# One block of scores moved one period ahead in a stick-breaking attention

## The chip, the cores and the metric

The kernel runs on one NeuronCore of a Trainium2 chip. The metric is the device time of one launch in microseconds (us). It is compared as a median of runs, and one further run was taken with the hardware profiler.

## The reference, cut to what matters

The kernel computes one layer of a decoder trunk on 1024 tokens of width 1024, all in 32-bit floats. It has a mixing sub-layer (stick-breaking attention beside a state-space mixer), a cross-attention and a feed-forward. The change is in the attention, which has 16 heads of width 64:

```python
for blk in range(seq // SB_BLOCK):               # 8 blocks of 128 rows
    t0 = blk * SB_BLOCK; t1 = t0 + SB_BLOCK
    z = einsum('bhtd,bhsd->bhts', qf[:, :, t0:t1], kf[:, :, :t1])
    causal = arange(t1)[None, :] < (t0 + arange(SB_BLOCK))[:, None]
    log_1mb = where(causal, log_sigmoid(-z), 0.0)
    tail = cumsum(log_1mb, axis=3, reverse=True)
    w = where(causal, exp(z + tail), 0.0)
    outs.append(einsum('bhts,bhsd->bhtd', w, vf[:, :, :t1]))
```

A block of 128 rows looks only at the keys up to its own end, so block 1 has 128 columns of scores, block 4 has 512, block 5 has 640 and block 8 has 1024.

## The kernel before, in words

Each head is worked off in two halves of four row blocks. A **short** half holds blocks 1 to 4 (128 to 512 columns), a **long** half holds blocks 5 to 8 (640 to 1024 columns). The 32 halves are numbered m = 0 to 31; even m is the short half of head m/2, odd m the long half of the same head.

For one row block, `scores` issues the score products on TensorE (L872, L873, in pieces of at most 512 columns into the three PSUM buffers `sc`), a sigmoid on ScalarE for each piece (L874, into the tile `n`), and one scan on VectorE over all the columns (L875). The `n` tiles of long halves come from a pool with four buffers, so a new block of a long half can be written only when the same block of the previous long half has been read for the last time.

For one half, `values` goes over key blocks i (four in a short half, eight in a long one). `tr(i)` transposes `n` on TensorE (L889, two PSUM buffers `tr`), ScalarE makes the high part `wth` (L892) and VectorE the low part `wtl` (L893). Three steps later `av(i)` multiplies both with the value differences (L901 with `wth`, L902 with `wtl`). So each L902 waits for a VectorE instruction.

A **period** m issues three things through `interleave`, which gives every item a place between 0 and 1 and sorts by it: the values of half m (over the whole period), the scores of half m+1 (over 0 to 0.7), and a quarter of the next two heads' q and k projections (`dense`, L104 to L106, spread over the whole period). In an even period the short values therefore stand beside the four long scans, and in an odd period the long values beside the four short ones.

This is the order in which the program is written. A scheduler places the instructions in each engine's queue by what it expects to be ready, and each queue then runs strictly in order. For two successive heads, first one with an even number and then one with an odd number, VectorE's queue holds the following. S5 to S8 are the long scans, s1 to s4 the short scans of the next head, w0 to w7 the `wtl` of the long values, v0 to v3 those of the short values after them, and gt and wlo the evacuation and the low weights of the projections:

```text
even head: w0 w1 w2 w3 gt S5 w4 w5 S6 S7 w6 w7 S8 s1 v0 s2 v1 wlo gt s3 v2 v3 s4
odd head:  w0 w1 w2 w3 gt S5 w4 w5 S6 S7 w6 w7 S8 s1 v0 v1 wlo gt s2 s3 v2 v3 s4
```

(In both rows S5 to S8 belong to the head after the one whose w's are listed.) ScalarE's sigmoids and TensorE's products stand in the order that this asks for. On GpSimd stand the value differences (`va`, L852, and their high and low parts, L94 and L101) and half of the high weights `whi`.

Of the kernel before, what the change touches and what calls it, by code (L numbers as in the profile page):

```python
# [34 lines left out]
def hybrid_block(ctx, tc, a, out, dbg=None):  # L35
# [13 lines left out]
    def mk(pl, shape, dt, tag, bufs=None):  # L49
        uid[0] += 1  # L50
        kw = {} if bufs is None else {"bufs": bufs}
        return pl.tile(shape, dt, tag=tag, name=f"{tag}_{uid[0]}", **kw)
# [202 lines left out]
    with ExitStack() as pa:  # L255
# [494 lines left out]
        with ExitStack() as p2:  # L750
# [85 lines left out]
            def gate_proj(gi):  # L836
                def ev(ps, half):
                    gt = mk(t2, [P, HALF], F32, "gt")
                    A.activation(gt, ps, AF.Sigmoid)
                    nc.sync.dma_start(g_d[gi * P:(gi + 1) * P, half * HALF:(half + 1) * HALF], gt)  # L840
                return dense(C_GA + gi * P, ev)
# [3 lines left out]
            def differences(h):  # L845

                j = h % 2
                if j == 0:
                    va, vb = [mk(vp, [P, NCH, P], F32, n, bufs=1) for n in ("va", "vb")]
                    for t, r in ((va, 0), (vb, 1)):  # L850
                        nc.sync.dma_start(t, v_d[r:S + r, h * HD:(h + 2) * HD].rearrange("(c p) d -> p c d", p=P))
                    G.tensor_tensor(va, va, vb, ALU.subtract)  # L852
                    dvs[0] = va
                dv = dvs[0][:, :, j * HD:(j + 1) * HD]
                vt = mk(vp, [P, NCH, P], F32R, "v")
                hi_sb(vt[:, :, 0:HD], dv, "p")
                lo_of(vt[:, :, HD:P], dv, vt[:, :, 0:HD], G)
                heads[h]["v"] = vt

            def scores(h, half, tb, ns_):  # L860
                def run():
                    hd = heads[h]
                    if half == 0 and tb == 0:
                        differences(h)
                    b = half * 4 + tb
                    L = (b + 1) * P
                    nt = mk(bp, [P, (half + 1) * HALF], F32, f"n{half}")
                    ns_.append(nt)
                    for s0 in range(0, L, HALF):
                        s1 = min(L, s0 + HALF)  # L870
                        ps = mk(psc, [P, HALF], F32, "sc")[:, :s1 - s0]
                        T.matmul(ps, hd["qs"][:, b * P:(b + 1) * P], hd["kh"][:, s0:s1], start=True, stop=False)  # L872
                        marks.append(T.matmul(ps, hd["qs"][:, b * P:(b + 1) * P], hd["kl"][:, s0:s1], start=False, stop=True))  # L873
                        sig.append(A.activation(nt[:, s0:s1], ps, AF.Sigmoid, scale=-(HD ** -0.5)))  # L874
                    V.tensor_tensor_scan(nt[:, 0:L][:, ::-1], nt[:, 0:L][:, ::-1], mask[:, S - L:][:, ::-1], 1.0, ALU.mult, ALU.max)  # L875
                return run
# [3 lines left out]
            def values(h, half, ns_):  # L880

                st = {}
                ni = 4 * (half + 1)

                def tr(i):
                    t0 = max(0, i - 4 * half)
                    pt = mk(pst, [P, HALF], F32, "tr")
                    for tb in range(t0, 4):
                        T.transpose(pt[:, tb * P:(tb + 1) * P], ns_[tb][:, i * P:(i + 1) * P], ident)  # L889
                    wh = mk(wt, [P, HALF], F32R, "wth")  # L890
                    wl = mk(wt, [P, HALF], F32R, "wtl")
                    A.activation(wh[:, t0 * P:], pt[:, t0 * P:], AF.Identity, bias=mone)  # L892
                    V.scalar_tensor_tensor(wl[:, t0 * P:], pt[:, t0 * P:], -1.0, wh[:, t0 * P:].bitcast(F32), ALU.add, ALU.subtract)  # L893
                    st[i] = (wh, wl, t0 * P)

                def av(i):
                    if i == 0:
                        st["po"] = mk(psv, [P, HALF], F32, "av")
                    po, vt = st["po"], heads[h]["v"]
                    wh, wl, off = st[i]  # L900
                    T.matmul(po[:, off:], vt[:, i, :], wh[:, off:], start=i == 0, stop=False)  # L901
                    marks.append(T.matmul(po[:, off:], vt[:, i, :], wl[:, off:], start=False, stop=i == ni - 1))  # L902
                    if i == ni - 1:
                        o = mk(t2, [P, HALF], F32, "oT")
                        A.activation(o, po, AF.Copy)
                        for j in range(2):
                            nc.sync.dma_start(o_d[j][h * HD:(h + 1) * HD, half * HALF:(half + 1) * HALF], o[j * HD:(j + 1) * HD])

                def step(i):
                    def run():  # L910
                        if i < ni:
                            tr(i)
                        if i >= LAG:
                            av(i - LAG)
                    return run

                return [step(i) for i in range(ni + LAG)]

            def interleave(*lists):
                items = []  # L920
                for n, (l, a0, a1) in enumerate(lists):
                    for i, f in enumerate(l):
                        items.append((a0 + (a1 - a0) * (i + 0.5) / len(l), n, f))
                for _, _, f in sorted(items, key=lambda t: t[:2]):
                    f()

            def qk_quanta(hp):

                if hp >= NH // 2:
                    return [[]] * 4  # L930
                q, k = qk_proj(hp)
                n = KT // FQ + 1
                return [q[:n], q[n:] + k[:1], k[1:n], k[n:]]
# [4 lines left out]
            NM = 2 * NH  # L938
            ns_ = {m: [] for m in range(NM)}
            nxt = qk_quanta(1)  # L940
            interleave(([scores(0, 0, tb, ns_[0]) for tb in range(4)], 0, 0.7), (nxt[0], 0, 1))
            late = [f for gi in range(16 - LATE_GATES, 16) for f in gate_proj(gi)]
            for m in range(NM):
                h, half = m // 2, m % 2
                hp, r = m // 4, m % 4
                s1 = [scores((m + 1) // 2, (m + 1) % 2, tb, ns_[m + 1]) for tb in range(4)] if m + 1 < NM else []
                if r == 3:
                    nxt = qk_quanta(hp + 2)
                dn = nxt[(r + 1) % 4]
                if m >= NM - 5:  # L950
                    n = -(-len(late) // (NM - m))
                    dn, late = late[:n], late[n:]
                interleave((values(h, half, ns_[m]), 0, 1), (s1, 0, 0.7), (dn, 0, 1))
            sig_last = sig[-1:]


# [946 lines left out]
```

## Time and profile before

| | us |
|---|---|
| median of 3 runs | 2558.97 |
| lowest, highest | 2551.43, 2560.34 |
| the profiled execution | 2557.21 |
| its span in the trace | 2555.4 |

The page of the profile gives the busy time of each engine: PE is TensorE's products, PEld its weight loads, DVE is VectorE, ACT is ScalarE, POOL is GpSimd, SP issues transfers. A group of instructions is given by its source line, engine, the tile written and the tile read, with the idle time of the engine ahead of it and the instruction that ended the idle time. Durations of products on PE overlap: the next one starts well before the last one's modelled end. In the timeline the columns are start, duration, engine, line, operation, tiles, shape and count, and in brackets the idle time ahead and what ended it.

The attention runs from about 666 us to 1088 us of the span.

### The profile page before, as it was taken

What the parts mean: (1) busy time and instruction counts of PE and PEld (TensorE: products, weight loads), DVE (VectorE), ACT (ScalarE), POOL (GpSimd) and SP (SyncE); (2) the same over time, 40 slices, a digit from 0 to 9 for tenths busy, and PEclk for the clock granted to TensorE, in tenths of its full rate; (3) what the DMA queues carried; (4) which work ended last, traced back from release to release, by engine and by line L of the source; (5) the groups of instructions that cost most, each with busy time, mean ns of one, the idle gap of its engine ahead of it and who ended that gap; (6) DMA issues with size and microseconds to landing.
All of it is one profiled execution on the core that took longest, in us unless ns stands there. A gap on an engine that the chain in (4) does not pass through costs nothing. (4 is left out here: it accounts for less than half of the span.)

```text
span 2555.4 us, 33383 instructions
## 1 busy us (share of the span) xinstructions
PE 2475.9 (97%) x12378; PEld 2033.6 (80%) x12378; DVE 1772.8 (69%) x2093; ACT 1133.7 (44%) x2023; POOL 853.9 (33%) x650
## 2 busy tenths in 40 slices
PE   7999999999999999999999999999999999999998
PEld 5788888887888878777777788887787888888876
DVE  7665777767578787688888664316459666666997
ACT  5333455555456665566554213215233333334343
POOL 3221544443121211256656040101113333323772
PEclk9999999999999999999999999999999999999999
DMA  7431443332543434365332662311232232224232
GB/s 246 152 116 55 138 149 99 99 112 90 153 112 87 120 99 104 100 207 168 107 106 65 203 209 83 124 50 34 99 116 66 83 91 75 90 91 165 99 132 99
DMA packets 255275, 293.51 MB, mean 115 GB/s; under 512 B 17023, under 2 KB 175240, under 8 KB 254986
## 3 DMA queue, kind: packets, MB, share of 16 engines
q1 hardware_dynamic: 255114, 291.40, 36.6%
q8 instruction: 97, 1.59, 0.3%
q14 instruction: 64, 0.52, 0.1%
HBM read 200.10 MB, written 74.45 MB: 107 GB/s over the span
## 5 line engine op out<-in xcount | busy, mean ns | idle before, releaser
L875 DVE TENSOR_TENSOR_SCAN n<-n,mask 128x128 f32<-128x128 f32 (+7 forms) x128 | 181.7, 1445 | 23.4 <-ACT n L874 22.2
L101 DVE TENSOR_TENSOR sw<-sf,sw 128x512 fp32r<-128x512 f32 x150 | 120.9, 818 | 82.0 <-ACT sw L98 80.5
L892 ACT ACTIVATE wth<-tr,mone 128x512 fp32r<-128x512 f32 x192 | 110.2, 584 | 81.4 <-PE tr L889 80.6
L98 ACT ACTIVATE sw<-sf 128x512 fp32r<-128x512 f32 x150 | 92.1, 626 | 113.0 <-PE mm L217 97.8
L183 POOL TENSOR_TENSOR sf<-wr,wr 128x512 f32<-128x512 f32 x38 | 59.4, 1563 | 233.4 <-DMA wr<-in_w_gu_dram 116.7
L893 DVE SCALAR_TENSOR_TENSOR wtl<-tr,wth 128x512 fp32r<-128x512 f32 x192 | 99.3, 544 | 53.9 <-ACT wth L892 53.8
L98 ACT ACTIVATE sw<-wr 128x512 fp32r<-128x512 f32 x113 | 71.2, 631 | 126.2 <-PE mm L217 125.6
L217 PE MATMUL mm<-h,sw 128*128 128x512 f32 x320 | 125.0, 392 | 1.8 <-DVE sw L101 1.8
L215 PE MATMUL mm<-h,sw 128*128 128x512 f32 x320 | 122.6, 391 | 2.9 <-ACT h L98 2.3
L216 PE MATMUL mm<-h,sw 128*128 128x512 f32 x320 | 125.3, 391 | 0.0
L101 DVE TENSOR_TENSOR sw<-wr,sw 128x512 fp32r<-128x512 f32 x113 | 106.6, 945 | 21.1 <-ACT sw L98 21.0
L669 DVE SCALAR_TENSOR_TENSOR b<-b,prmT,b 128x1023 f32<-128x1023 f32 (+2 forms) x72 | 109.6, 1522 | 15.1 <-ACT b L667 14.5
L94 POOL TENSOR_SCALAR v<-va 128x512 fp32r<-128x512 f32 x16 | 20.6, 1289 | 278.2 <-PE av L902 164.0
L874 ACT ACTIVATE n<-sc 128x512 f32<-128x512 f32 (+1 forms) x192 | 88.6, 494 | 45.5 <-PE tr L889 28.8
L152 POOL TENSOR_SCALAR rstd<-ms 128x1 f32<-128x1 f32 x74 | 28.1, 379 | 237.1 <-ACT x L1414 110.3
L104 PE MATMUL mm<-oth,bw 128*128 128x512 f32 x256 | 103.6, 405 | 3.6 <-DVE a L1214 3.6
L104 PE MATMUL p<-bw,h 128*128 128x512 f32 x256 | 98.7, 391 | 3.3 <-DVE x L1416 2.4
L105 PE MATMUL mm<-otl,bw 128*128 128x512 f32 x256 | 100.5, 393 | 0.0
L106 PE MATMUL mm<-oth,bw 128*128 128x512 f32 x256 | 100.4, 392 | 0.0
L106 PE MATMUL p<-bw,h 128*128 128x512 f32 x256 | 100.1, 392 | 0.0
L105 PE MATMUL p<-bw,h 128*128 128x512 f32 x256 | 99.9, 390 | 0.0
L185 POOL TENSOR_TENSOR sf<-wr 128x512 f32<-128x512 f32 x38 | 63.0, 1657 | 105.4 <-DVE sw L101 105.4
(616 smaller groups left out, 8044.0 us busy)
## 6 DMA issues: line engine op xcount, KB each, us to landing
wr<-in_w_gu_dram SPq DMA_DIRECT2D x80, 256.0 KB
wr<-in_w_in_dram SPq DMA_DIRECT2D x36, 512.0 KB
zr<-in_w_in_dram SPq DMA_DIRECT2D x28, 512.0 KB
gu_d<-t SPq DMA_DIRECT2D x44, 256.0 KB
wraw<-in_w_in_dram SPq DMA_DIRECT2D x20, 512.0 KB
zs_d<-zo SPq DMA_DIRECT2D x32, 256.0 KB
xs_d<-b SPq DMA_DIRECT2D x32, 256.0 KB
kl<-gt SPq DMA_DIRECT2D x64, 128.0 KB
```

The source lines that it names most:

```text
L98: A.activation(o, i, AF.Copy)
L101: eng.tensor_tensor(o, i, hi.bitcast(F32), ALU.subtract)
L104: first = T.matmul(ps, sh, mh, start=start, stop=False)
L105: T.matmul(ps, sh, ml, start=False, stop=False)
L106: T.matmul(ps, sl, mh, start=False, stop=stop)
L215: T.matmul(ps, w[0][:, k, :], bh, start=first and k == 0, stop=False, skip_group_check=True)
L216: T.matmul(ps, w[0][:, k, :], bl, start=False, stop=False, skip_group_check=True)
L217: ins = T.matmul(ps, w[1][:, k, :], bh, start=False, stop=last and k == 3, skip_group_check=True)
L669: V.scalar_tensor_tensor(acc[:, sh:], y[:, :S - sh], cw(3 - sh, f), acc[:, sh:], ALU.mult, ALU.add)
L875: V.tensor_tensor_scan(nt[:, 0:L][:, ::-1], nt[:, 0:L][:, ::-1], mask[:, S - L:][:, ::-1], 1.0, ALU.mult, ALU.max)
L892: A.activation(wh[:, t0 * P:], pt[:, t0 * P:], AF.Identity, bias=mone)
L893: V.scalar_tensor_tensor(wl[:, t0 * P:], pt[:, t0 * P:], -1.0, wh[:, t0 * P:].bitcast(F32), ALU.add, ALU.subtract)
```

## The change

The first row block of each long half (block 5, with its 640 columns) is taken out of the four blocks that an even period issues, and is issued one period sooner, in the last 30% of the odd period before, beside the short scans and the long values. The other three long blocks are spread over the same stretch as the four were. For the very first long half the block goes beside the first short scans.

```diff
-            interleave(([scores(0, 0, tb, ns_[0]) for tb in range(4)], 0, 0.7), (nxt[0], 0, 1))
+            interleave(([scores(0, 0, tb, ns_[0]) for tb in range(4)], 0, 0.7), ([scores(0, 1, 0, ns_[1])], 0.75, 1), (nxt[0], 0, 1))
 ...
-                s1 = [scores((m + 1) // 2, (m + 1) % 2, tb, ns_[m + 1]) for tb in range(4)] if m + 1 < NM else []
+                s1 = [scores((m + 1) // 2, (m + 1) % 2, tb, ns_[m + 1]) for tb in range(1 - half, 4)] if m + 1 < NM else []
+                s2 = [scores((m + 2) // 2, 1, 0, ns_[m + 2])] if half and m + 2 < NM else []
 ...
-                interleave((values(h, half, ns_[m]), 0, 1), (s1, 0, 0.7), (dn, 0, 1))
+                interleave((values(h, half, ns_[m]), 0, 1), (s1, 0, 0.7), (s2, 0.7, 1), (dn, 0, 1))
```

No instruction is added or removed. With the change the scheduler fills VectorE's queue like this, in the notation of above:

```text
even head: w0 w1 w2 w3 S5 w4 gt S6 w5 w6 S7 w7 S8 v0 wlo gt s1 v1 s2 s3 v2 v3 s4
odd head:  w0 w1 w2 w3 S5 w4 gt S6 w5 w6 S7 w7 S8 v0 s1 v1 wlo gt s2 s3 v2 v3 s4
```

On TensorE the last score pieces of blocks 7 and 8 now stand behind 12 or 13 projection products, instead of being mixed with them, and the last transposition `tr(7)` directly behind them. Behind `tr(7)` stand, with the number of 512-column products in figures:

```text
even head: tr7 avlo5 avhi6 avlo6 tr0 6 sc1 2 av7 tr1 sc2 sc3 sc4 tr2 avhi0 avlo0 6 avhi1 sc5 tr3 avlo1 avhi2 avlo2
odd head:  tr7 avlo5 avhi6 avlo6 tr0 2 sc1 av7 tr1 9 sc2 sc3 sc4 avhi0 tr2 avlo0 avhi1 3 tr3 avlo1 3 sc5 avhi2 sc6 avlo2
```

tr0 to tr3 and the last av0 to av2 belong to the short values that follow; each sc is a pair of products. GpSimd's queue puts each `whi` ahead of the value parts that it stood behind. The queue of transfers keeps its order but for one key move per two heads, which goes ahead of an output store. Outside the attention the scheduler places some transpositions of the cross-attention's output stage (L165) up to ten products later; nothing else moves.

## The prediction

> **What bounds the kernel now.** I read the page first, then the busy times of the attention's stretch, then who waits for whom there, and last the timeline of two periods.
>
> ```profile
> span 2555.4 us, 33383 instructions
> PE 2475.9 (97%) x12378; PEld 2033.6 (80%) x12378; DVE 1772.8 (69%) x2093; ACT 1133.7 (44%) x2023; POOL 853.9 (33%) x650
> ...
> 643.00:664.00 21.00, 21.00 (x94) 17.41 (x93) 3.30 (x4) 5.51 (x10) 8.89 (x7) 1.00 0.79 230
> 664.00:1065.00 401.00, 391.94 (x2109) 325.91 (x2108) 301.02 (x353) 235.49 (x472) 66.28 (x46) 1.00 0.38 99
> ```
>
> The last two rows are stretches of time: length, then busy time of PE, PEld, DVE, ACT and POOL, and the granted clock (1.00 in both). In the attention (664 to 1065 us) PE is busy 391.94 of 401 us, DVE 301. So PE sets the length, and since the change adds and removes no instruction, it can only change what PE waits for. The 9 us that PE idles there are the first measure of what can be gained; the loss has no such limit.
>
> [...]
>
> ```profile
> PEld av L902 <- DVE wtl L893: 10.2, 14, 1.4
> DVE wlo L101 <- POOL whi L94: 7.0, 8, 1.1
> PE av L902 <- DVE wtl L893: 7.3, 6, 1.2
> PE av L901 <- ACT wth L892: 2.5, 1, 2.5
> PE tr L889 <- DVE wtl L893: 1.8, 4, 0.5
> ```
>
> These are waits over 666 to 1088 us: total, times, longest. PE's waits are nearly all one kind: a product with the low part waits for VectorE. On PE's own row it shows six times for 1.2 us each. The weight load of the same product shows it 14 times with 10.2 us in all, because PE's modelled ends cover the start of each wait. I take 10.2 us as the whole price. The timeline shows where one of the six comes from:
>
> ```profile
> 745.52 1.49 DVE L875 TENSOR_TENSOR_SCAN n<-n,mask 128x640 f32<-128x640 f32 x1
> 746.93 1.13 DVE L893 SCALAR_TENSOR_TENSOR wtl<-tr,wth 128x512 fp32r<-128x512 f32 x2
> 747.97 3.66 DVE L875 TENSOR_TENSOR_SCAN n<-n,mask 128x768 f32<-128x768 f32 x2
> 751.55 0.59 DVE L893 SCALAR_TENSOR_TENSOR wtl<-tr,wth 128x256 fp32r<-128x256 f32 x2
> 752.07 2.97 DVE L875 TENSOR_TENSOR_SCAN n<-n,mask 128x1024 f32<-128x1024 f32 x2
> 754.96 0.66 DVE L893 SCALAR_TENSOR_TENSOR wtl<-tr,wth 128x512 fp32r<-128x512 f32 x1
> 755.54 1.16 DVE L875 TENSOR_TENSOR_SCAN n<-n,mask 128x256 f32<-128x256 f32 x1
> ...
> 757.97 1.23 DVE L101 TENSOR_TENSOR wlo<-wraw,whi 128x1024 fp32r<-128x1024 f32 x1 [0.82 <-POOL whi L94]
> 759.11 0.68 DVE L827 TENSOR_TENSOR gt<-mm,kh 128x512 fp32r<-128x512 f32 x1
> ```
>
> ```profile
> 748.61 0.40 PE L105 MATMUL mm<-t1l,whi 128*128 128x512 f32 x1
> 748.85 0.39 PE L106 MATMUL mm<-t1h,wlo 128*128 128x512 f32 x1
> ...
> 750.44 0.33 PE L901 MATMUL av<-wth,v 128*128 128x256 f32 x1
> 752.00 0.38 PE L902 MATMUL av<-wtl,v 128*128 128x256 f32 x1 [1.23 <-DVE wtl L893]
> ...
> 752.29 0.62 PE L889 MATMUL tr<-ident,n 128*128 128x128 f32 x4
> 752.66 0.48 PE L104 MATMUL mm<-t1h,whi 128*128 128x512 f32 x1
> ```
>
> S6 and S7 (the row of 3.66 us) stand back to back on DVE, w6 only behind them, and avlo6 at 752.00 waits for w6. It is the long scans that are late in this place, not the long values.
>
> **The change, part by part.**
>
> *The block's own place.* In both queues S5 follows w3: its four-buffer pool gives the slot free when tr4 has read it, and that hardly moves. So issuing the block a period sooner does not make it run a period sooner; it shifts the neighbours. The score products wait in PSUM as they did. The costs of the move itself (two pairs of products, two sigmoids, one 1.49 us scan) are the same work: zero. It issues no transfer: the loads of the values hang on the first block of the short half.
>
> *What goes.* With the change S6 stands ahead of w5 and w6, S7 behind them. Between w6 and avlo6 PE now has the 13 projection products that stand ahead of the last score pieces: 13 x 0.23 us (748.61 to 748.85) = 3.0 us. S6, w5 and w6 (1.7 of the 3.66 us, then 0.45 and 0.3 us) run beside them, and behind them PE still has three more projection products and two pairs of score pieces, some 2 us, before avlo6. All of the waits of avlo6, six long and seven or eight short ones, go: 10.2 us. The cover is those 13 (12 in an odd head) products; without them about 1 us of wait would be back.
>
> *What is late next.* The same 13 products delay the last pieces of S7 and S8. Everything behind S8 on DVE comes later, seen from PE: v0, wlo, gt, s1, v1, s2, s3, v2. On PE avlo2 of the short values waits for v2, and ahead of it the small transpositions wait for v0 and v1 to free their PSUM buffers. I walk both queues from the start of tr7, at clock 0.
>
> ```profile
> L874 ACT ACTIVATE n<-sc 128x512 f32<-128x512 f32 x77 | 44.9, 600 | 15.4 <-PE tr L889 14.8 <-PE sc L873 0.2
> L892 ACT ACTIVATE wth<-tr,mone 128x128 fp32r<-128x128 f32 x25 | 9.3, 371 | 17.4 <-PE tr L889 17.4
> L893 DVE SCALAR_TENSOR_TENSOR wtl<-tr,wth 128x384 fp32r<-128x384 f32 x25 | 13.5, 540 | 0.0
> L875 DVE TENSOR_TENSOR_SCAN n<-n,mask 128x128 f32<-128x128 f32 x12 | 9.2, 771 | 0.0
> ...
> 778.24 2.98 DVE L875 TENSOR_TENSOR_SCAN n<-n,mask 128x1024 f32<-128x1024 f32 x2 [0.31 <-ACT n L874]
> ...
> 784.55 1.53 DVE L875 TENSOR_TENSOR_SCAN n<-n,mask 128x256 f32<-128x256 f32 x2
> 786.00 0.59 DVE L893 SCALAR_TENSOR_TENSOR wtl<-tr,wth 128x256 fp32r<-128x256 f32 x2
> 786.51 3.12 DVE L875 TENSOR_TENSOR_SCAN n<-n,mask 128x512 f32<-128x512 f32 x1
> ...
> 778.62 0.51 PE L889 MATMUL tr<-ident,n 128*128 128x128 f32 x3
> ...
> 787.27 0.28 PE L902 MATMUL av<-wtl,v 128*128 128x256 f32 x1
> ```
>
> ScalarE: behind tr7 one wth of 0.37 us and two sigmoids of 0.60 us. With 0.3 us for tr7 itself and overlaps of 0.1 us, S8 starts at 1.8 us. DVE, even head, each with its duration less 0.1 us of overlap: S8 2.2 (to 4.0), v0 0.6 (4.6), wlo 1.15 (5.7), gt 0.6 (6.3), s1 0.7 (7.0), v1 0.45 (7.5), s2 and s3 1.45 (8.9), v2 0.4: 9.3 us. In an odd head the order differs and the sum is the same: 9.3 us.
>
> PE, even head, at 0.23 us for 512 columns, smaller ones in proportion, 0.11 us for a transposition and 0.08 us more for the product behind one (0.48 at 752.66 against 0.40): up to avlo6 0.5; tr0 0.5; eight projection products 1.85; sc1 and av7 0.25; tr1 0.35; sc2 to sc4 1.1; tr2 0.2; avhi0, avlo0 0.55; six products 1.4; avhi1 0.15; sc5 0.45; tr3 0.1; avlo1 0.25; avhi2 0.1. That is 7.75 us, and 0.25 us more because tr2 and tr3 arrive 0.1 us ahead of the end of v0 and of v1. PE is at avlo2 at 8.0 us and waits 1.3 us. PE, odd head: nine products more ahead of sc2, sc5 and sc6 ahead of avlo2, by the same prices 9.05 us; it waits 0.25 us. Before, S8 of such a head started 0.4 us ahead of tr1 (778.24, 778.62) and v2, at 786.40, was 0.9 us ahead of avlo2 (787.27). By the walk S8 starts 0.1 us behind tr1, PE needs 1.3 us less from tr1 to avlo2 (7.3 against 8.65 us), and DVE 0.65 us less from S8 to v2 (7.5 against 8.15 us): 0.5 + 1.3 - 0.65 is 1.15 us later against 0.9 us to spare, again 0.25 us. With PE's sum 0.4 us off it would be 0.65 us; I take 0.45 us there.
>
> Bounds: s2 can cost 0.5 us more (1.16 us at 755.54; at 784.55 it and s3 together take 1.53 us), and the PE sums carry some 0.4 us each. So one pair of heads pays between 1.3 and 2.9 us; my value is 1.3 + 0.25 + 0.45 = 2.0 us. The wait for `whi` (7.0 us over 8 times) lay ahead of wlo and shortens, since whi goes ahead of the value parts on POOL; it is inside the walk as zero. Behind whi the value parts are queued, and no product waits for them in the list of waits.
>
> *The queue of transfers* keeps its order but for the one key move; the late pieces of the keys are evacuated at about the same place of the period. I put it at zero, between -0.5 and +1 us. *The L165 transpositions* have no wait in PE's list of waits over the whole span: zero, at most 1 us when the feed-forward starts.
>
> *The end of the attention* has a wait that can swallow a loss:
>
> ```profile
> 1084.64 0.63 ACT L98 ACTIVATE ch<-cfm 128x512 fp32r<-128x512 f32 x1 [3.05 <-DMA cfm<-cf_d]
> ```
>
> ScalarE waits 3.05 us for a transfer of the next stage, and PE behind it 2.5 us (the row of L901 above). If the attention gets there later and the transfer does not, up to 2.5 us of loss vanish. The transfer is issued behind output stores of the attention, so I count nothing.
>
> **The sum.** Six regular pairs of heads: -10.2 + 6 x 2.0 = +1.8 us. The profiled execution took 2557.21 us, so 2559.0 us in its terms. The median of the runs, 2558.97, lies 1.76 us above it, which gives 2560.8 us. With the bounds (6 x 1.3 to 6 x 2.9, -0.5 to +2 for the rest, 2.5 swallowed or not) this case reaches from 2553.5 to 2568.
>
> **The rivals.**
>
> *Nothing takes the place of the wait.* Then the 10.2 us are gained: 2548.8 us. For it speaks that DVE is only 75% busy, and that the change takes two long scans apart. Against it: the chain behind S8 is counted from rows, and the row at 786.00 shows that it has 0.9 us to spare at most. [...]
>
> *POOL gets in front of a scan that PE waits for.* Slower.
>
> ```profile
> 786.16 2.39 POOL L852 TENSOR_TENSOR va<-va,vb 128x1024 f32<-128x1024 f32 x1 [3.83 <-DMA va<-v_d]
> ...
> 761.12 1.22 DVE L875 TENSOR_TENSOR_SCAN n<-n,mask 128x512 f32<-128x512 f32 x1
> ```
>
> The 512-column scan takes 1.22 us alone, but 3.12 us at 786.51, where POOL's subtraction (786.16) had started: DVE stands still for 1.9 us. There it hit s4, behind v2. The point of decision is 1.0 us: if the subtraction starts that much sooner against DVE's chain, it hits s3, and v2, for which PE already waits, is 1.9 us later. Once in each of seven pairs that is 13.3 us: 2574.1 us. For it: the chain after S8 moves, and by more than the transfer that releases the subtraction. Against it: the subtraction hangs on the last product of the odd head's long values, as S8 nearly does, and by the walk both move within 0.5 us. [...]
>
> *The change does nothing.* The slot freed by tr4 fixes S5, and the rest stays as it is: 2559.0 us. For it: S5 keeps its place behind w3. Against it: the order of S6, w5, w6 and S7 does change.
>
> **How the numbers follow.** Chances: forecast 0.60, nothing in its place 0.16, POOL 0.12, no effect 0.12. A measurement of this kernel can tell about 0.5%, 12.8 us, from no change. Only POOL's case passes that (+15.1 us), with a little from the forecast's upper end, and more than 12.8 us of gain would need waits that the trace does not show. So slower 0.13, faster 0.03, same 0.84. The range runs from the first rival's 2548.8, rounded out, to the second's 2574: 2548 to 2574 us.
>
> **What would show it.** After: L902's waits for `wtl` at 256 columns should stand in the short values (behind S8, wlo, gt and three short scans, 1.0 to 1.6 us in every even head) and not behind two long scans. S6 and S7 should stand singly on DVE. PE's idle total in the attention should be within 4 us of before. It is wrong if DVE shows v2 in time for avlo2, or if scans of 256 or 384 columns show up at twice their duration.

## The result, and the profile after

| | before | after |
|---|---|---|
| median of 22 runs, us | 2557.71 | 2561.13 |
| lowest, highest, us | 2551.43, 2560.52 | 2552.24, 2565.49 |
| mean granted clock of the runs | not on record | 0.9922 |
| the profiled execution, us | 2557.21 | 2552.24 |
| its granted clock | 0.992 | 0.994 |

The ratio is 1.0015, with a 95% interval of 1.0009 to 1.0020: 3.8 us slower (2.3 to 5.1), which is no change within 0.5%. The forecast was +1.8 us.

The profiled execution of after happens to be its fastest run, and that of before one of its slower ones, so the two spans can't be subtracted. The attention can be compared by itself. Of the page and of the stretch that the prediction showed, and of the waits over 660 to 1090 us (total, times, longest):

```profile
span 2550.4 us, 33410 instructions
...
PE 2468.3 (97%) x12378; PEld 2030.3 (80%) x12378; DVE 1772.4 (69%) x2093; ACT 1129.8 (44%) x2023; POOL 871.8 (34%) x650
```

```profile
664.00:1065.00 401.00, 386.31 (x2079) 322.65 (x2078) 296.82 (x350) 231.26 (x469) 82.90 (x46) 0.99 0.36 96
```

```profile
PEld av L902 <- DVE wtl L893: 14.3, 14, 1.4
PEld tr L889 <- DVE wtl L893: 11.6, 16, 1.3
PE av L902 <- DVE wtl L893: 9.6, 14, 1.1
...
PE tr L889 <- DVE wtl L893: 6.2, 9, 0.9
...
PE av L901 <- ACT wth L892: 1.4, 1, 1.4
```

PE is busy 386.31 us of the stretch instead of 391.94: the waits have not gone, they have grown. On PE's own row L902 waits 9.6 us instead of 7.3, and the transpositions 6.2 us instead of 1.8. The wait at the end (L901) fell from 2.5 to 1.4 us. The granted clock of the stretch is 0.99 instead of 1.00. From the first score product to the last L902 product the attention takes 426.6 us instead of 421.5 (660.0 to 1086.6 and 666.3 to 1087.8).

The place of the waits is the one that the prediction named. These are rows of PE, then of VectorE and GpSimd, in one even head of after; the number in brackets is the wait ahead of the row:

```profile
754.03 0.40 PE L873 MATMUL sc<-kl,qs 128*128 128x512 f32 x1
755.29 0.33 PE L889 MATMUL tr<-ident,n 128*128 128x128 f32 x1 [0.87 <-DVE wtl L893]
...
757.05 0.39 PE L902 MATMUL av<-wtl,v 128*128 128x256 f32 x1 [1.14 <-DVE wtl L893]
```

```profile
748.56 2.29 DVE L875 TENSOR_TENSOR_SCAN n<-n,mask 128x1024 f32<-128x1024 f32 x1 [0.55 <-ACT n L874]
750.77 0.67 DVE L893 SCALAR_TENSOR_TENSOR wtl<-tr,wth 128x512 fp32r<-128x512 f32 x1
751.74 1.62 DVE L101 TENSOR_TENSOR wlo<-wraw,whi 128x1024 fp32r<-128x1024 f32 x1 [0.30 <-POOL whi L94]
753.28 0.68 DVE L827 TENSOR_TENSOR gt<-mm,kh 128x512 fp32r<-128x512 f32 x1
753.88 0.90 DVE L875 TENSOR_TENSOR_SCAN n<-n,mask 128x128 f32<-128x128 f32 x1
754.71 0.53 DVE L893 SCALAR_TENSOR_TENSOR wtl<-tr,wth 128x384 fp32r<-128x384 f32 x1
755.16 1.52 DVE L875 TENSOR_TENSOR_SCAN n<-n,mask 128x256 f32<-128x256 f32 x2
756.61 0.59 DVE L893 SCALAR_TENSOR_TENSOR wtl<-tr,wth 128x256 fp32r<-128x256 f32 x2
...
749.02 2.68 POOL L94 TENSOR_SCALAR whi<-wraw 128x1024 fp32r<-128x1024 f32 x1 [13.45 <-PE mm L105]
...
752.37 2.14 POOL L101 TENSOR_TENSOR v<-va,v 128x512 fp32r<-128x512 f32 x1
```

Read VectorE from the top: S8, v0, wlo, gt, s1, v1, s2 with s3, v2 with v3. tr3 at 755.29 waits for v1 (it ends at 755.24), avlo2 at 757.05 for v2 (listed singly, v2 takes 0.39 us and ends at 757.00). Each even head from 706 to 963 us shows these two waits, each odd head one of 0.23 us.

One more thing is new. The windows of 4 us around that place end with the granted clock, the DMA share and GB/s:

```profile
752.00:756.00 4.00, 3.04 (x14) 2.04 (x12) 4.00 (x6) 1.05 (x4) 2.42 (x2) 1.00 0.62 148
756.00:760.00 4.00, 2.95 (x12) 2.66 (x13) 3.02 (x5) 1.28 (x4) 0.00 (x0) 0.67 0.77 225
760.00:764.00 4.00, 4.00 (x22) 3.50 (x21) 0.69 (x1) 1.62 (x3) 0.00 (x0) 0.91 0.28 66
```

Behind the pair of waits the clock falls to half for some 3.4 us: 4 x (0.33 + 0.09) = 1.7 us of clock are lost. This follows two of the six pairs of waits in the profiled run.

### The profile page after: what moved, and what is told of

It reads as the page before. It is cut to its first block, busy times and chain, and to the rows that moved or that the text cites. A ratio compares the mean times of both kernels' runs of the same rounds, so it can differ in the third digit from the quotient of the medians.

```text
span 2550.4 us, 33410 instructions
## 1 busy us (share of the span) xinstructions
PE 2468.3 (97%) x12378; PEld 2030.3 (80%) x12378; DVE 1772.4 (69%) x2093; ACT 1129.8 (44%) x2023; POOL 871.8 (34%) x650
## 5 line engine op out<-in xcount | busy, mean ns | idle before, releaser
L875 DVE TENSOR_TENSOR_SCAN n<-n,mask 128x128 f32<-128x128 f32 (+7 forms) x128 | 175.0, 1378 | 44.6 <-ACT n L874 43.9
L874 ACT ACTIVATE n<-sc 128x512 f32<-128x512 f32 (+1 forms) x192 | 87.7, 491 | 50.6 <-PE sc L873 45.2
L889 PE MATMUL tr<-ident,n 128*128 128x128 f32 x576 | 96.2, 278 | 6.2 <-DVE wtl L893 6.2
```

## The experiments

Theory T: the change takes the wait of avlo6 away and lengthens, as PE sees it, the chain on VectorE behind S8 (v0, wlo, gt, s1, v1, s2, s3, v2), and the waits on that chain are the whole loss. Rivals: the loss lies elsewhere (R1), GpSimd stands in VectorE's way (R2). All comparisons are with before on the same chip in the same stretch of time.

| | changed | ratio to before, 95% | us | attention, us |
|---|---|---|---|---|
| after | | 1.0015 (1.0009 to 1.0020) | +3.8 | 426.6 |
| e1 | after, wlo on GpSimd | 1.0094 (1.0077 to 1.0111) | +24.0 | 443.6 |
| e2 | before, wlo on GpSimd | 1.0025 (1.0016 to 1.0033) | +6.4 | 425.5 |
| e3 | change for even heads only | 0.9981 (0.9972 to 0.9989) | -4.9 | 420.2 |
| e4 | change for odd heads only | 1.0015 (1.0003 to 1.0026) | +3.8 | 424.9 |
| e5 | after, wlo later | 0.9968 (0.9956 to 0.9979) | -8.2 | 414.4 |
| e6 | before, wlo later | 1.0038 (1.0026 to 1.0051) | +9.7 | 433.0 |
| e7 | after, fifth n buffer | 1.0034 (1.0022 to 1.0047) | +8.7 | 431.1 |
| e8 | e6, subtraction on VectorE | 0.9993 (0.9985 to 1.0002) | -1.8 | 423.4 |
| e9 | e7, subtraction on VectorE | 0.9978 (0.9969 to 0.9986) | -5.6 | 419.1 |
| e10 | e9 and wlo later | 0.9960 (0.9945 to 0.9974) | -10.2 | 413.3 |
| e11 | before, subtraction on VectorE | 0.9997 (0.9988 to 1.0006) | -0.8 | 421.3 |
| e12 | e5, subtraction on VectorE | 0.9961 (0.9950 to 0.9973) | -10.0 | 413.7 |

The last column is the attention in the profiled execution (421.5 in before), the fourth the ratio's distance from 1 times the median of before. Less before's 421.5 it agrees with the fourth within 3.7 us over a spread of 34 us. This speaks against R1 where the difference is clearly larger than that; for e3, e8 and e9 it decides nothing.

**e1 and e2: wlo on GpSimd.**

```diff
-        lo_of(lo, raw, hi)
+        lo_of(lo, raw, hi, G if rb == 1 else V)
```

> The changed kernel with the low weights of the projections (wlo, half of the raw weights less their high part) subtracted on GpSimd instead of VectorE. Theory T (the wait has moved behind S8): in the trace of after, VectorE in an even head ends v0 at 751.44 us, then waits 0.30 us for whi, takes 1.62 us for wlo and starts gt at 753.28. Without wlo the chain to v1 and v2 is 1.84 us shorter, and the two waits behind it (0.87 us of tr3 at 755.29, 1.14 us of avlo2 at 757.05) fall from 2.0 to about 0.2 us. The odd head's 0.23 us go too: 6 x (1.84 + 0.23) = 12.4 us less than after, 0.9966 of before. Rival R1 (the loss of the change lies outside these waits, in the later stages or the clock): within 2 us of after, 1.001 to 1.002 of before. Rival R2 (GpSimd stands in VectorE's way): the subtraction of 2.1 us, as of the low value part at 752.37, falls on the short scans, which stretch by up to its length; the gain is eaten up and the kernel is at 1.0015 of before or above, with short scans at twice their duration in the trace.

> The same move of wlo to GpSimd in the kernel before. Theory T: there the waits of the products are those of avlo6 for w6 (6 x 1.2 us on PE's own row), which stand ahead of wlo on VectorE, and v2 has 0.9 us to spare; so wlo is hidden and nothing is gained: within 2 us of before (0.9992 to 1.0008). Rival R1b (wlo on VectorE costs PE time in both kernels alike): 7 to 12 us less, 0.995 to 0.997. Rival R2 (GpSimd's subtraction stretches scans by about 2 us in each head): 1.002 or above.

VectorE, then GpSimd, in e1:

```profile
814.33 2.53 DVE L875 TENSOR_TENSOR_SCAN n<-n,mask 128x128 f32<-128x128 f32 x1
816.77 0.53 DVE L893 SCALAR_TENSOR_TENSOR wtl<-tr,wth 128x384 fp32r<-128x384 f32 x1
817.22 2.55 DVE L875 TENSOR_TENSOR_SCAN n<-n,mask 128x256 f32<-128x256 f32 x2
...
814.17 2.40 POOL L101 TENSOR_TENSOR wlo<-wraw,whi 128x1024 fp32r<-128x1024 f32 x1
...
817.35 1.61 POOL L101 TENSOR_TENSOR v<-va,v 128x512 fp32r<-128x512 f32 x1
```

R2 wins. GpSimd starts wlo 0.16 us ahead of s1, and s1 with its 128 columns takes 2.53 us, where the same scan takes 0.90 in after; it ends 0.3 us behind wlo. So the work taken off VectorE comes back in the scan (called the lock below: the scan, which started second, takes longer, and ends behind GpSimd's subtraction; s4 at 786.51 in before took 3.12 us instead of 1.22 and ended 1.08 us behind the subtraction), avlo2 waits 2.2 us instead of 1.14, and the clock falls behind five of the six pairs of waits:

```profile
816.00:820.00 4.00, 1.42 (x7) 0.72 (x5) 4.00 (x5) 0.85 (x2) 2.87 (x3) 0.92 0.67 160
820.00:824.00 4.00, 3.86 (x16) 3.57 (x16) 2.11 (x4) 1.26 (x2) 0.00 (x0) 0.50 0.51 139
```

The runs of e1 have a mean clock of 0.988 against 0.9937 beside them, worth some 14 of the 24 us (a fall lasts 3.4 us or twice that there). In e2 the lock shows twice: a 384-column scan takes 2.35 us beside wlo (0.93 alone), and the value subtraction on GpSimd now starts ahead of s4 in all six pairs (s4 takes 2.83 to 3.06 us). What PE gains in waits there stands behind s4: a transposition waits 0.65 to 0.87 us in each pair, while the six waits of avlo6 stay at 1.2 us. T's "nothing" was a miss there too. As a test of the chain e1 is void: it did not shorten it.

**e3 and e4: half of the change.**

```diff
-  ... for tb in range(1 - half, 4)] if m + 1 < NM else []
+  ... for tb in range(1 if not half and h % 2 == 0 else 0, 4)] if m + 1 < NM else []
-  s2 = [scores((m + 2) // 2, 1, 0, ns_[m + 2])] if half and m + 2 < NM else []
+  s2 = [...] if half and m + 2 < NM and (h + 1) % 2 == 0 else []
```

(e3; e4 has 1 for 0, and leaves the first long half as before. In the order of VectorE the blocks of even heads stand behind the w's of odd heads, and the reverse.)

> The change for the long halves of even heads alone; the long blocks of odd heads are issued as before. These are the scans that stand behind the w's of odd heads (the row 'odd head' of VectorE's queue). Theory T: in before that row has hardly a wait (0.2 us once per pair, on the weight load), in after it has 0.23 us for avlo2: 6 x 0.23 = 1.4 us more, of which the transfer at the end can swallow 1.1 us. 1.0000 to 1.0006 of before. Rival R1 (the loss is spread over the kernel, not tied to these waits): half of the +3.8 us, 1.0007.

> The change for the long halves of odd heads alone (the scans that stand behind the w's of even heads, the row 'even head' of VectorE's queue). Theory T: there the 1.2 us of avlo6 in each pair go and 0.87 + 1.14 us come: 6 x 0.8 = 4.9 us more, less up to 1.1 us at the end: 1.0015 to 1.0020 of before, the whole loss of the change. Rival R1: half of the +3.8 us, 1.0007. A third reading, that the whole 10.2 us of the weight-load row count as the price of avlo6: 6 x (2.0 - 1.7) = 1.8 us more, 1.0007 as well.

Waits of e3, then rows of e4:

```profile
PE av L902 <- DVE wtl L893: 7.6, 7, 1.2
...
PE tr L889 <- DVE wtl L893: 1.2, 3, 0.5
```

```profile
838.39 3.33 DVE L875 TENSOR_TENSOR_SCAN n<-n,mask 128x512 f32<-128x512 f32 x1
...
838.24 2.40 POOL L852 TENSOR_TENSOR va<-va,vb 128x1024 f32<-128x1024 f32 x1 [4.03 <-DMA va<-v_d]
...
814.99 0.33 PE L872 MATMUL sc<-kh,qs 128*128 128x128 f32 x1 [1.48 <-DMA kh<-kh]
```

The loss lies in e4's half, as T says. Its size fits T, but the interval also holds the 1.0007 of R1 and of the third reading, and the fit is partly luck, as e4 gets there by other waits than T's: tr3 waits only 0.2 us, s4 is locked out in five of six pairs (3.33 us here) and a transposition behind it waits 0.9 to 1.2 us, and once PE waits for a key transfer. e3 was a miss to the good side: 4.9 us less, where 0 to 1.4 us more was expected. Its waits are those of before, so the trace explains 1.3 us (its attention) and no more. The rest stays open.

**e5 and e6: wlo held back.** wlo stays on VectorE, but is tied to a product that was issued ten marks earlier, so that it goes behind s4, where VectorE idles in after:

```diff
-  st["w"] = load_split(wp, colblock(w_in, c0), [P, KT, P], 1)
+  (load raw, make hi as before)
+  low = V.tensor_tensor(lo, raw, hi.bitcast(F32), ALU.subtract)
+  if len(marks) >= 10:
+      issue_behind(low, marks[-10])
```

> The changed kernel with wlo kept on VectorE but held back to a place behind s4, where VectorE idles for 2.5 us (0.72 at 759.04 and 1.78 at 761.52 in the trace of after); the products that use it come a quarter of the projections later. Nothing else moves but a few score and projection products by one place. Theory T (the wait of the change is the chain behind S8): the chain is 1.84 us shorter in an even head, so 0.87 + 1.14 us of waits become about 0.2 us, and the odd head's 0.23 us go: 6 x 2.07 = 12.4 us less than after. The two stretches of half clock, 3.4 us each, that follow this pair of waits in after's profile should go too, 1.7 us each: 0.995 to 0.997 of before. Rival R1 (the loss of the change is elsewhere): 1.001 to 1.002, as after. Rival R4 (VectorE's chain was only the last of several that end together, and the next one, ScalarE's wth or the scores in PSUM, holds PE as long): 0.999 to 1.001, with new waits of tr or L901 for ScalarE.

> The same holding back of wlo in the kernel before. Theory T: its waits are those of avlo6 for w6, which stands ahead of wlo, so they stay (7.3 us on PE's own row), and nothing is gained but the 0.3 to 0.5 us waits of tr twice: 0.9990 to 1.0005. Rival R1b (wlo in that place costs PE time whatever the order of the long scans): 0.995 to 0.997.

Waits of e5, its stretch, and PE at the place of the two waits:

```profile
PE av L902 <- DVE wtl L893: 5.0, 8, 1.0
PE tr L889 <- DVE wtl L893: 2.8, 10, 0.6
```

```profile
664.00:1065.00 401.00, 393.79 (x2137) 330.70 (x2136) 301.28 (x361) 239.72 (x484) 84.59 (x51) 1.00 0.39 102
```

```profile
808.60 0.39 PE L902 MATMUL av<-wtl,v 128*128 128x256 f32 x1 [0.60 <-DVE wtl L893]
```

This is the clean test, and T holds: 12.0 us less than after (12.4 expected from the waits, 15.8 with the two falls of the clock in after's profile), the wait of tr3 is gone, avlo2 waits 0.60 instead of 1.14 us, and the clock of the stretch is 1.00 again. So the change does free time, and the chain behind S8 had taken it. In e6, however, the same edit costs 9.7 us instead of nothing. GpSimd, VectorE and PE there (L774 is wlo):

```profile
787.54 2.38 POOL L852 TENSOR_TENSOR va<-va,vb 128x1024 f32<-128x1024 f32 x1 [4.09 <-DMA va<-v_d]
787.61 3.39 DVE L875 TENSOR_TENSOR_SCAN n<-n,mask 128x512 f32<-128x512 f32 x1
...
790.92 1.20 DVE L774 TENSOR_TENSOR wlo<-wraw,whi 128x1024 fp32r<-128x1024 f32 x1
792.04 1.28 DVE L893 SCALAR_TENSOR_TENSOR wtl<-tr,wth 128x512 fp32r<-128x512 f32 x2
...
792.77 0.44 PE L889 MATMUL tr<-ident,n 128*128 128x128 f32 x2 [1.64 <-DVE wtl L893]
```

The value subtraction starts 0.07 us ahead of s4, s4 takes 2.2 us longer, wlo comes behind it, and a transposition waits for w0. In before it was the other way round in four of six pairs; here by 0.03 us:

```profile
836.49 1.21 DVE L875 TENSOR_TENSOR_SCAN n<-n,mask 128x512 f32<-128x512 f32 x1
836.52 3.36 POOL L852 TENSOR_TENSOR va<-va,vb 128x1024 f32<-128x1024 f32 x1 [4.21 <-DMA va<-v_d]
```

**e7: a fifth buffer for the long tiles.**

```diff
-  nt = mk(bp, [P, (half + 1) * HALF], F32, f"n{half}")
+  nt = mk(bp, [P, (half + 1) * HALF], F32, f"n{half}", bufs=4 + half)
```

> The changed kernel with five buffers instead of four for the long blocks' tiles n, so that S5 needs no slot freed by tr4. The prediction's step says that this slot, not the place of issue, fixes S5: then in VectorE's queue S5 now stands ahead of w0 or w1 instead of behind w3, S6 and S7 move up by as much, and the last pieces of S8 stand three projection products and two short score pairs ahead of tr7 (some 1.1 us) instead of directly ahead of it. Theory T: the chain behind S8 starts 1.1 us sooner against PE, in even heads 1.1 us of the 2.0 us of waits go, 6 x 1.1 = 6.6 us less than after: 0.9985 to 0.9995 of before. Rival R1: as after, 1.001 to 1.002. Rival R5 (the block that now runs a period sooner pushes the short scans back, and the waits grow): above 1.003.

S5 does move, to behind w0 and in the next head to behind s4: the slot had fixed it. But the time was a miss, 1.0034. The lock again:

```profile
787.22 2.39 POOL L852 TENSOR_TENSOR va<-va,vb 128x1024 f32<-128x1024 f32 x1 [4.03 <-DMA va<-v_d]
...
787.65 4.43 DVE L875 TENSOR_TENSOR_SCAN n<-n,mask 128x512 f32<-128x512 f32 x2
...
792.72 0.55 PE L889 MATMUL tr<-ident,n 128*128 128x128 f32 x3 [1.68 <-DVE wtl L893]
```

The row of 4.43 us holds s4 and S5; listed singly s4 takes 3.05 us of it. In three other pairs the subtraction meets S5, which takes 3.62 us instead of 1.49.

**e8 to e12: the value subtraction on VectorE.**

```diff
-  G.tensor_tensor(va, va, vb, ALU.subtract)      # at the first short block
+  issue_behind(V.tensor_tensor(va, va, vb, ALU.subtract), scan)   # behind the scan of the last one
```

The high and low value parts, which stay on GpSimd, are issued there too, behind the subtraction.

> The kernel of e6 (before, wlo held back behind s4) with the value subtraction of two heads (L852, 128x1024 from two tiles in SBUF) on VectorE behind the last short scan of an even head, instead of on GpSimd when its transfer lands. In e6 GpSimd starts it 0.07 us ahead of s4 of the odd head (787.54 against 787.61), s4 takes 3.39 us instead of 1.21, wlo stands behind it, and a transposition waits 1.64 us on PE; so in nearly all pairs. Theory P (GpSimd and VectorE lock each other out for a whole instruction, and who starts first decides): s4 is 1.21 us in all heads, the 1.6 us waits go, 6 x 1.6 = 9.8 us less than e6: 0.9995 to 1.0010 of before. Rival R6 (it is wlo's new place ahead of w0 that costs, lock or not): 1.003 to 1.004, with the waits of tr still there.

> The kernel of e7 (the change, five n buffers) with the same move of the value subtraction to VectorE. In e7 it locks out s4 or the S5 that now follows it (3.05 to 3.62 us instead of 1.21 and 1.49), and a transposition behind waits 1.7 to 2.0 us in each pair of heads. Theory P: these waits go, 6 x 1.8 = 10.8 us less than e7, and with them the half clock that followed one: 0.9985 to 0.9998 of before, where the expectation of e7 had it. Rival R5 (S5 a period sooner pushes the long values back by its own 1.49 us): 1.002 to 1.003.

> All three together on the changed kernel: five n buffers, wlo held back (here ahead of v3 and s4), the value subtraction on VectorE. If the gains add: e5's 0.9968, less the 0.60 and 0.35 us per pair that are left there (6 x 0.95 = 5.7 us): 0.9945 to 0.9965. If S5 behind s4 takes the idle time that wlo and the subtraction need (0.72 + 1.78 us in after, against 1.49 + 1.2 us), the first transpositions of the long values wait by what is over: 0.997 to 0.999.

Waits of the transpositions in e8, then in e9:

```profile
PE tr L889 <- DVE wtl L893: 2.6, 4, 1.3
```

```profile
PE tr L889 <- DVE wtl L893: 2.9, 4, 1.6
```

In e6 and e7 they were 11.6 and 12.3 us. The lock is shown as the cause: with the subtraction on VectorE e6 falls by 11.5 us to before's time, and e7 by 14.3 us, a little further than the expectations of e7 and e9 had it. e10, with all three edits, is at 0.9960, within its first range, but the gains overlap: from after, the fifth buffer with the moved subtraction is worth 9.4 us (e9), holding back wlo 12.0 us (e5), and all three together 14.0 us.

> The kernel before with the value subtraction on VectorE behind the last short scan of an even head, and nothing else; it asks what the lock costs there, and with that why e3 came out 4.9 us faster where 0 to 1.4 us slower was expected. In before's profile the subtraction starts within 0.1 us of s4 in four of six pairs, and ahead of it in the two others (786.16 and 935.83), where s4 takes 3.12 and 3.26 us and a transposition waits 0.32 and 0.5 us on PE; in e3 it never starts ahead. Theory P1 (these short waits are all that the lock costs): 2 x 0.4 = 0.8 us less, 0.9995 to 0.9999, and e3 stays unexplained. Theory P2 (the lock is hit by chance in more pairs in other runs, and what it pushes back costs more than the wait that the profile names): the pairs of heads take 49.6 us each, as in e3 and e8, instead of 49.5 to 51.0 (mean of five 50.2), 6 x 0.6 = 3.6 us less: 0.998 to 0.999.

> The kernel of e5 (the change, wlo held back) with the value subtraction on VectorE, without the fifth n buffer of e10. Theory P: in e5 the subtraction always starts behind s4, so there is no lock to be taken away, and 1.2 us more on VectorE behind s4 of each even head fit into the 2.5 us that it idles there less the 1.2 us of wlo: 0.9963 to 0.9975, as e5. Rival: the two together delay w0 in even heads and a transposition waits up to 1 us once per pair: 0.998 to 0.999.

e11 came out where P1 has it: in before the lock costs hardly more than the waits that its trace shows (P2's mildest value, 0.999, lies just inside the interval). So the lock explains little of e3. e12 shows that the fifth buffer adds nothing to the other two: 0.9961. e5, e10 and e12 beat both kernels; among the three the intervals overlap.

## Why the prediction was right, and which terms were off

*S5 is fixed by its slot.* Right: VectorE's order in after keeps it behind w3, and e7, which gives a slot, moves it.

*What goes: the waits of avlo6, 10.2 us.* Right in kind: no long value with 256 columns waits in after. In size it can't be read singly. e5, in which what came instead is mostly gone, gained 8.2 us; and e12, which is e8 with the change, lies 8.2 us below e8 (-10.0 against -1.8), with the lock gone and wlo held back in both. So some 8 of the 10.2 us show.

*What is late next.* The place was right, wait by wait. The size in an even head: avlo2 1.3 forecast, 1.14 measured; tr2 and tr3 0.25 in all forecast, 0.87 measured for tr3 alone. In an odd head 0.45 forecast, 0.23 measured. A pair therefore pays 2.24 us instead of 2.0. That avlo2's wait came out so near is partly luck: from the start of tr7 (746.88), v2 ends after 10.1 us instead of the 9.3 of the walk, PE gets to avlo2 after 8.2 us without its waits instead of 7.75, and tr3 pays part of the difference.

The mis-sized step is the walk of VectorE from v0 to v1, where the wait for `whi` stood "inside the walk as zero". It is 0.30 us (0.82 in before), wlo takes 1.62 instead of the 1.23 us of before, and s1 0.90 instead of 0.77 us. From S8's start to v2's end it is 8.44 us (748.56 to 757.00) where the walk had 7.5, and these three make up most of the difference. While whi goes ahead of the value parts, as the prediction says, the value part at 752.37 now runs on GpSimd beside wlo, gt and s1; that it lengthens these two is likely from e1, but was not tried alone.

*The term left out is the clock.* The forecast counted each wait once. In the profiled execution of after two stretches of half clock cost 1.7 us each, and before has none in the same stretch. The pairs of heads tell the two terms apart: from one wait of avlo2 to the next after takes 50.6 us where no half clock lies between (three times), and 52.1 and 52.3 us where it does; before takes 49.5 to 50.5 us from one wait of avlo6 to the next, 50.0 in the mean. So the exchange of waits costs 0.65 us per pair, or 3.9 us over six, where the forecast had 1.8; the clock costs some 3 us more in this execution. In the sum over PE's rows the waits grow by 5.6 us (9.6 + 6.2 + 1.4 against 7.3 + 1.8 + 2.5), so the terms do not add up exactly. How often the clock falls in the other runs is not on record, and neither is the clock of before's runs beside them. The forecast's +1.8 us lies just under the interval (2.3 to 5.1); the longer chain alone is large enough to make the difference, and whether the clock has a part in it stays open.

*The end of the attention* swallowed 1.1 of the possible 2.5 us; it had been counted as nothing.

*The rivals.* That nothing takes the wait's place: refuted by the waits, though e5 shows that the 10 us were there to be had. GpSimd ahead of a scan: it did not happen in after, where the subtraction starts 0.48 to 0.86 us behind s4's start in all six pairs; the rival was real all the same, as e4, e6 and e7 ran into it, by margins of 0.07 to 0.5 us. That the change does nothing: refuted by the order and by e3 and e4. PE's idle time in the stretch grew by 5.6 us, where the prediction had allowed 4.

## What to carry to other kernels

When a change takes a wait away, list the whole queue of the engine that was waited for, up to the next instruction that another engine needs, and look in it for work that nobody needs soon: here wlo, due a quarter of the projections later, stood in that chain, and moving it was worth three times the change's loss. Check a scan and a subtraction on GpSimd by their starting times and not their lengths: with a subtraction that started 0.03 us behind it s4 took 1.21 us (before), with one 0.07 us ahead 3.39 us (e6). Add up waits of the bound engine that lie within a few microseconds of each other, and look at the granted clock behind them: here 2.01 and 1.76 us of idle time in 3.4 us were followed by half clock, which cost 1.7 us more each time.

## What the runs showed of the hardware

*The lock.* A scan of 512 columns takes 1.21 us, also where the subtraction starts 0.03 us behind it (which then takes 3.36 us instead of 2.39; before, 836.52); where the subtraction starts 0.07 us ahead, the scan takes 3.39 (e6, 787.61). A scan of 128 columns took 2.53 us where wlo started 0.16 us ahead (e1, 814.33).

*Half clock behind short waits.* Waits of 0.87 and 1.14 us within 2.6 us were followed by half clock for 3.4 us in two of six pairs of after, waits of 0.56 and 2.17 us (e1) for 3.4 or 6.8 us in five of six; a single wait of 1.2 us in before, e3 or e8 never was in the same stretch. The two falls of after begin at 757.33 and 859.73 us and last 3.41 us each; from one to the other it is 102.40 us, 30 times 3.413 us. Cut from the first fall into windows of that length, with the windows that hold most of a pair of waits, and those of the two falls, after shows (length, PE's busy time, granted clock, DMA share, GB/s):

```profile
702.71:706.12 3.41, 1.76 (x9) 1.00 0.68 179
753.91:757.33 3.42, 1.41 (x8) 1.00 0.80 229
757.33:760.74 3.41, 3.41 (x15) 0.50 0.46 121
856.31:859.73 3.42, 1.66 (x8) 1.00 0.68 184
859.73:863.14 3.41, 3.16 (x12) 0.50 0.62 178
958.71:962.13 3.42, 1.94 (x10) 1.00 0.75 175
```

PE idles for 2.01 and 1.76 us of the windows ahead of the two falls, and for 1.65, 1.48 or less of those of the four other pairs, which these windows cut in two. Half clock for 3.4 us came behind a single long wait too (1.81 us in e6, 2.02 us in e7). What makes the clock fall is not shown.
